# Row scales of a decoder trunk: sums over the partitions by two matmuls with a matrix of ones, and a power over 512 columns

## The chip, the cores and the metric

The kernel runs on one core of a Trainium2 chip. The metric is the device time of one execution in microseconds (us); of several executions the median is taken. Engines are named as in the profile: PE is TensorE's matmul, PEld its weight load, DVE is VectorE, ACT is ScalarE, POOL is GpSimd, SP is SyncE. L198 is line 198 of the kernel before.

## What is computed

A trunk of two decoder layers over 512 tokens with 1024 features. Each layer is a half-step SwiGLU feed-forward, a token mixer (a gated linear recurrence in the first layer, latent attention in the second), another half-step SwiGLU, and a gated embedding. An RMS norm stands ahead of every one of these, and one at the end:

```
def _rmsnorm(x, g):
    x32 = x.astype(jnp.float32)
    y = x32 * lax.rsqrt(jnp.mean(x32 * x32, axis=-1, keepdims=True) + EPS)
    return (y * g.astype(jnp.float32)).astype(x.dtype)

for li in range(DEPTH):
    g = norm_gains[li]
    x = x + 0.5 * _swiglu(_rmsnorm(x, g[0]), ffn_w_in[li, 0], ffn_w_out[li, 0])
    h = _rmsnorm(x, g[1])
    x = x + (hgrn2 mixer of h in layer 0, latent attention of h in layer 1)
    x = x + 0.5 * _swiglu(_rmsnorm(x, g[2]), ffn_w_in[li, 1], ffn_w_out[li, 1])
    gate = sigmoid(_rmsnorm(x, g[3]) @ ple_w_gate[li])
    x = x + gate * (p[li] @ ple_w_in[li])
    if li == 0:
        shared = _mla_shared_kv(x, positions, ...)   # norm, down projection, norm of 256 latents
return _rmsnorm(x, final_norm)
```

The norm's factor is one number for each token, 1/sqrt(mean of squares + EPS). Everything that follows a norm is linear until the next nonlinearity, so the kernel multiplies by the gain first, does the matmuls, and applies the factor of the token to their result.

## The kernel before, in words

**Layout.** Activations stand transposed: features on the 128 partitions, the 512 tokens along the free axis. A tensor of 1024 features is eight tiles of 128x512. A token's sum of squares is therefore a sum over the partitions and over eight tiles. The eight tiles are summed elementwise as they come (class `Stats`, L176; the squares on ACT at L183, the additions on POOL or DVE at L188). What is left is one 128x512 tile whose 128 rows must be summed.

**Matmuls.** An f32 product is made of three matmuls of halves (`mm3`, L150): each operand is split into a rounded high part `hi` (a cast on ACT, `split` L166, or L304 for weights) and the rest `lo` (a subtraction on DVE, L167, L305). Weights stream from memory in tiles of 128x1024, eight blocks of 128x128. A chain over eight blocks is 24 matmuls of 128x512 into one PSUM bank. There are eight banks: four of tag `mm` (`mm_bank`, L92) and four of tag `aux` (`aux_bank`, L95), each given out in turn, so a fifth chain on `mm` needs the first one's bank read out.

**The row factor.** `column_sums` (L211) turns the 128x512 tile by four transposes on PE (L214) into a bank, and DVE adds along the free axis (L216), which leaves 128x4: the 512 sums, one column for each 128 tokens. `Stats.columns` adds EPS on DVE (L195) and raises to the power -0.5 on POOL (L198, 128x4). `spread` (L219) broadcasts each of the four columns and transposes it back on PE (L222), and `rows` (L225) copies the bank to a tile `rb` of 128x512 on ACT (L229): each partition holds the same 512 factors. Consumers multiply a bank by `rb` on DVE, and by that free the bank.

**Where it stands.** Eight places make `rb` in this way and are touched by the change:
1. at the very start, for the first feed-forward, whose first two gate and up products are made ahead, into all four `mm` banks (`primed`, L1227);
2. to 4. at the opening of the other three feed-forwards (`plain`, L399): eight products of 24 matmuls into the `mm` banks in turn, the sums after product 0, the spread after product 1, the copy (`fresh`, L425) at the start of product 2, and then `gated` and `kept` (L387, L393), which read out two banks each time;
5. and 6. ahead of the two gated embeddings (`ple` L901 and `last` L919): eight short chains of six matmuls, then eight gate chains of 24, each read out by a multiplication with `rb` at L911;
7. the norm of the 256 shared latents (`shared`, L1036), which is worked off in steps beside the third feed-forward's first output stage;
8. ahead of the latent attention (`mla`, L1067): four chains of 24, each read out by a multiplication with `rb` at L1074 into `cq`.

A ninth place, the recurrence, uses the 128x4 form itself and stays as it was, as do the recurrence's heads, the queries' norm and the final norm.

**What sets the order.** Within a feed-forward the order on every engine is as written: `turn` (L359) takes weight tile t, does what is due at t, cuts (L299 and L304 on ACT, L300 and L305 on DVE) the tile two turns ahead, and issues the loads some turns ahead. From the fifth feature block on, pairs of blocks are multiplied with fewer products: class `Mix` (L247) prepares sums of activation halves on DVE (L262) and POOL (L264, L265), and some weight tiles are added in memory on the way in by DMAs that POOL issues (L288). Outside the feed-forwards a scheduler sets the order when the kernel is built. Each engine works through its own queue in order.

Of the kernel before, what the change touches and what calls it, by code (L numbers as in the profile page):

```python
# [28 lines left out]
EPS = 1e-6  # L29
# [28 lines left out]
def kernel(  # L58
# [12 lines left out]
    act, dve, pool, pe = nc.scalar, nc.vector, nc.gpsimd, nc.tensor  # L71
# [14 lines left out]
    def slot(s="s", dt=F32, tag="s"):  # L86
        return spool.tile([P, T], dt, tag=tag, bufs=BUFS[tag], name=name(s))
# [4 lines left out]
    def mm_bank():  # L92
        return psum.tile([P, T], F32, tag="mm", bufs=4, name=name("mm"))

    def aux_bank():  # L95
        return psum.tile([P, T], F32, tag="aux", bufs=4, name=name("aux"))
# [11 lines left out]
    ones = cpool.tile([P, 1], F32, name="ones")  # L108
    dve.memset(ones, 1.0)
    jmat = cs[:, C_J : C_J + P]  # L110


    stream = {"n": 0, "tiles": 0, "ready": [], "now": None}
# [49 lines left out]
    def split(src, scale=None, tag="s"):  # L163
        hi, lo = slot("hi", F32R, tag), slot("lo", F32R, tag)
        if scale is None:
            act.copy(hi, src)  # L166
            dve.tensor_tensor(out=lo, in0=src, in1=hi.bitcast(F32), op=ALU.subtract)  # L167
        else:
            act.activation(hi, src, AF.Copy, scale=scale)
            dve.scalar_tensor_tensor(  # L170
                out=lo, in0=src, scalar=scale, in1=hi.bitcast(F32), op0=ALU.mult, op1=ALU.subtract
            )
        return hi, lo
# [37 lines left out]
    def column_sums(src):  # L211
# [4 lines left out]
        dve.tensor_reduce(out=r, in_=pt.rearrange("p (j q) -> p j q", j=NT), axis=AX.X, op=ALU.add)  # L216
        return r

    def spread(r):  # L219
        pb = aux_bank()  # L220
        for j in range(NT):
            pe.transpose(pb[:, j * P : (j + 1) * P], r[:, j : j + 1].to_broadcast([P, P]), ident)  # L222
        return pb

    def rows(stats, sums=None):  # L225
        r = stats.columns(sums)
        pb = spread(r)
        rb = slot("rb", F32, "b")
        act.copy(rb, pb)  # L229
        return r, rb  # L230


    x = [slot("x") for _ in range(KC)]
# [86 lines left out]
    def ffn(nx, post, rb=None, primed=(), aside=None, ready=None):  # L320
# [27 lines left out]
        def at(dt, fn, late=False):  # L348
            todo.setdefault((now[0] + dt, late), []).append(fn)
# [49 lines left out]
        def plain(f0):  # L399
            xg = nx.xg[0]  # L400
            mixed = [Mix(nx, i) for i in range(KC // 2)]
            n = 2 * (PLAIN - f0)
            if f0:
                for i in range(KC // 2):
                    if i == 0:
                        mixed[0].scale()
                        mixed[0].combine()
                        mixed[0].cut(b)
                        mixed[1].scale()
                    else:  # L410
                        at(i - 1, mixed[i].combine)
                        at(i, lambda i=i: mixed[i].cut(b), True)
                        if i < KC // 2 - 1:
                            at(i - 1, mixed[i + 1].scale, True)
            else:
                for i in range(KC // 2):
                    at(max(2 * i - 1, 0), mixed[i].scale, i > 0)
                    at(2 * i, mixed[i].combine, i == 0)
                    at(2 * i + 1, lambda i=i: mixed[i].cut(b), True)
            ps = [None] * n  # L420
            r = pb = None

            def fresh():
                st["rb"] = slot("rb", F32, "b")
                act.copy(st["rb"], pb)  # L425

            for t in range(n):
                f = f0 + t // 2
                if t == 2 and not f0:
                    at(0, fresh)  # L430
                if t % 2 == 0 and t > 0:
                    at(0, lambda t=t: st.update(g=gated(ps[t - 2])))
                    at(0, lambda t=t: kept(ps[t - 1], st["g"]), True)
                if t == 2 and not f0 and ready is not None:
                    at(0, lambda: ready(st["rb"]), True)
                w = turn()
                ps[t] = aux_bank() if f0 and t < 2 else mm_bank()
                full(ps[t], w, xg, range(KC), True, True)
                if t == 0 and not f0:
                    r = nx.stats.columns(nx.stats.sums())  # L440
                if t == 1 and not f0:
                    pb = spread(r)
                now[0] += 1
            at(0, lambda: st.update(g=gated(ps[n - 2])))
            at(0, lambda: kept(ps[n - 1], st["g"]))

# [589 lines left out]
    def shared(sh, sin, cos, out):  # L1036
        tab = slot("tab", F32, "r")
        act.copy(tab[0:64, :], cos[0:64, :])
        act.activation(tab[64:128, :], sin[64:128, :], AF.Copy, scale=cs[64:128, C_SIGN : C_SIGN + 1])
        kt = slot("kt", F32, "r")  # L1040
        dve.tensor_tensor(out=kt, in0=sh.kr, in1=tab, op=ALU.mult)
        st = Stats(2)
        for c in sh.lat:
            st.add(c)
        yield
        pj = aux_bank()
        pe.matmul(pj, jmat, kt, start=True, stop=True)
        sums = st.sums()
        r = st.columns(sums)
        krope = split(pj, None, "p")  # L1050
        yield
        pb = spread(r)
        rc = slot("rb", F32, "b")
        act.copy(rc, pb)
        yield
        cn = []
        for m in range(2):
            c = slot("cn", F32, "r")
            dve.scalar_tensor_tensor(
                out=c, in0=sh.lat[m], scalar=gain(V_LAT, m), in1=rc, op0=ALU.mult, op1=ALU.mult  # L1060
            )
            cn.append(split(c, None, "p"))
            yield
        out.extend((cn, krope))


    def mla(xg, stats, cn, krope, sin, cos, post):  # L1067
        _, rb = rows(stats)
        st = Stats(4, dve)
        cq = []  # L1070
        for m in range(4):
# [156 lines left out]
    with tc.manual_schedule(engines={mybir.EngineType.SP, mybir.EngineType.PE}):  # L1228
        warm = tiny(1)
        act.activation(warm, ones, AF.Square)  # L1230
        nc.sync.dma_start(vc, vec)
        load(0)
        for i in range(4):
            stream["tiles"] += 1
            stream["n"] += WB
            raw = wpool.tile([P, WB * P], F32, tag="raw", bufs=5, name=name("raw"))
            hi = wpool.tile([P, WB * P], F32R, tag="whi", bufs=3, name=name("whi"))
            lo = wpool.tile([P, WB * P], F32R, tag="wlo", bufs=3, name=name("wlo"))
            for e in range(2):
                m = 2 * i + e  # L1240
                s = slice(e * WB * P // 2, (e + 1) * WB * P // 2)
                if i == 0:
                    nc.sync.dma_start(raw[:, s], wall[i][:, s])
                    load(m + 1)
                elif e == 0:
                    nc.sync.dma_start(raw, wall[i])
                    for k in range(m + 1, min(m + 3, KC)):
                        load(k)
                first(m)
                for n in range(2) if m == 0 else (None,):  # L1250
                    c = s if n is None else slice(s.start + n * 2 * P, s.start + (n + 1) * 2 * P)
                    act.copy(hi[:, c], raw[:, c])  # L1252
                    dve.tensor_tensor(out=lo[:, c], in0=raw[:, c], in1=hi[:, c].bitcast(F32), op=ALU.subtract)
                if m == 5:
                    nc.sync.dma_start(cs, cst)
                first.stats.add(x[m])
                if m == KC - 1:
                    sums = first.stats.sums()
                for c in range(4):
                    w = slice(s.start + c * P, s.start + (c + 1) * P)  # L1260
                    mm3(primed[c], (hi[:, w], lo[:, w]), first.xg[0][m], m == 0, m == KC - 1)
        rb = rows(first.stats, sums)[1]
    tables, held = [], []
    n1 = Next([gcol(0, 1)])

# [13 lines left out]
    n3 = Next([gcol(0, 3)])  # L1279
    ffn(n2, n3, aside=embedding(0))  # L1280
    n4 = Next([gcol(1, 0)])
    rb = rows(n3.stats)[1]
    sh = Shared()

    def both(m):
# [12 lines left out]
    mla(n5.xg[0], n5.stats, cn, krope, sin, cos, n6)  # L1298
    n7 = Next([gcol(1, 3)])
    ffn(n6, n7, aside=embedding(1))  # L1300
    last(n7.xg[0], held[1], rows(n7.stats)[1])


def _blocks(w):
# [166 lines left out]
```

## Time and profile before

| | |
|---|---|
| median of 3 runs | 2176.32 us (2176.1 to 2176.52) |
| profiled execution, own time | 2175.48 us |
| its span | 2173.7 us |
| granted TensorE clock, mean | 0.997 |
| busy: PE, DVE, ACT, POOL | 99%, 70%, 45%, 14% of the span |
| instructions on PE | 13026 |

The profile shows one execution. Its span runs from the first to the last recorded instruction; its own time is 1.8 us longer. "Busy" is the time in which an engine executes an instruction, and a duration is an instruction's own: matmuls are pipelined, so one of 128x512 shows 0.39 us while the next starts 0.23 us after it. "Idle before" is how long the engine had waited, with the instruction that ended it.

### The profile page before, as it was taken

Reading aid. Unit: us, or ns where it says so; the run is one execution under the profiler, and the core shown is the slowest. Engines: PE = TensorE matmul, PEld = TensorE weight load, DVE = VectorE, ACT = ScalarE, POOL = GpSimd, SP = SyncE. Lnnn points to the kernel's source line nnn. Section 1 sums busy time; section 2 is a strip of 40 time slices with the busy share of each in tenths; the row PEclk is TensorE's granted clock in tenths of the full one; section 3 lists DMA queues with packets and bytes.
Section 4 is the critical chain, followed back from the end, with each engine's and each line's share of the span. In section 5 each row is a group of like instructions: output and inputs, shape, how many; then the busy total and the mean of one; then the engine's idle time right before and its main releaser. Section 6 shows DMA issues by size and latency. Waiting matters only on the chain.

```text
span 2173.7 us, 32746 instructions
## 1 busy us (share of the span) xinstructions
PE 2148.8 (99%) x13026; PEld 1925.5 (89%) x13026; DVE 1522.3 (70%) x2261; ACT 968.5 (45%) x1374; POOL 313.3 (14%) x428
## 2 busy tenths in 40 slices
PE   8999999999999999999999999999999999999998
PEld 7899998898888899998888989988888888999987
DVE  6776676777786676675767757767676776775765
ACT  6354453223235343344553525446444563443543
POOL 2000001554521000001110000011110110000011
PEclk9999999999999999999999999999999999999999
DMA  5555552211123555552244655423122134654631
GB/s 192 141 157 159 144 163 96 83 69 59 68 69 105 147 159 159 141 160 101 87 119 127 172 146 157 144 91 104 59 85 91 51 105 132 151 164 126 178 104 49
DMA packets 76249, 261.46 MB, mean 120 GB/s; under 512 B 9152, under 2 KB 11328, under 8 KB 76096
## 3 DMA queue, kind: packets, MB, share of 16 engines
q1 hardware_dynamic: 64864, 220.15, 30.4%
q0 software_dynamic: 10368, 37.75, 10.1%
q8 instruction: 102, 1.67, 0.3%
q10 hardware_dynamic: 864, 1.46, 0.2%
q14 instruction: 51, 0.42, 0.1%
HBM read 253.04 MB, written 2.10 MB: 117 GB/s over the span
## 4 chain that ended last, share of the span: by engine, by line
PE 94%; DVE 3%; ACT 1%; issue 1%; DMA 0%; POOL 0%; SPq 0%; POOLq 0%; DVEq 0%; ACTq 0%
PE aux L314 19%; PE mm L151 18%; PE mm L152 18%; PE mm L153 17%; PE mm L314 14%; PE aux L152 1%; PE aux L153 1%; PE aux L723 1%; PE aux L151 1%; PE aux L1163 1%; PE aux L1138 0%; PE aux L1137 0%; ACT whi L304 0%; PE aux L214 0%; DVE wlo L305 0%
## 5 line engine op out<-in xcount | busy, mean ns | idle before, releaser
L151 PE MATMUL mm<-hi,whi 128*128 128x512 f32 x1656 | 647.1, 393 | 8.5 <-ACT whi L1252 5.6
L152 PE MATMUL mm<-lo,whi 128*128 128x512 f32 x1656 | 647.2, 391 | 1.5 <-DVE lo L380 0.9
L153 PE MATMUL mm<-hi,wlo 128*128 128x512 f32 x1656 | 646.1, 390 | 0.0
L305 DVE TENSOR_TENSOR wlo<-raw,whi 128x1024 fp32r<-128x1024 f32 x340 | 425.3, 1251 | 220.6 <-ACT whi L304 217.5
L304 ACT CAST whi<-raw 128x1024 fp32r<-128x1024 f32 x340 | 355.2, 1046 | 288.3 <-PE mm L152 163.5
L151 PEld LDWEIGHTS mm<-hi,whi 128*128 128x128 f32 x1656 | 311.3, 188 | 72.2 <-ACT whi L1252 5.6
L152 PEld LDWEIGHTS mm<-lo,whi 128*128 128x128 f32 x1656 | 311.7, 188 | 64.1 <-DVE lo L380 2.2
L153 PEld LDWEIGHTS mm<-hi,wlo 128*128 128x128 f32 x1656 | 311.5, 188 | 63.4
L314 PE MATMUL aux<-hi,whi 128*128 128x256 f32 x1152 | 328.1, 285 | 2.5 <-ACT mm L465 2.5
L314 PE MATMUL aux<-hi,wlo 128*128 128x256 f32 x1152 | 326.8, 284 | 0.2 <-DVE wlo L300 0.2
L314 PE MATMUL aux<-lo,whi 128*128 128x256 f32 x1152 | 326.5, 283 | 0.0
L314 PE MATMUL mm<-lo,whi 128*128 128x256 f32 x864 | 244.5, 283 | 0.0
L314 PE MATMUL mm<-hi,whi 128*128 128x256 f32 x864 | 244.5, 283 | 0.0
L314 PE MATMUL mm<-hi,wlo 128*128 128x256 f32 x864 | 244.4, 283 | 0.0
L314 PEld LDWEIGHTS aux<-hi,whi 128*128 128x128 f32 x1152 | 221.6, 192 | 3.3 <-ACT mm L465 2.7
L314 PEld LDWEIGHTS aux<-hi,wlo 128*128 128x128 f32 x1152 | 221.7, 192 | 0.5 <-DVE wlo L300 0.5
L314 PEld LDWEIGHTS aux<-lo,whi 128*128 128x128 f32 x1152 | 221.6, 192 | 0.5
L288 POOL DMA_DIRECT2D raw<-in_wall x72 | 62.8, 872 | 941.1 <-DMA raw<-in_wall 538.5
L129 ACT CAST whi<-raw 128x1024 fp32r<-128x1024 f32 x95 | 99.8, 1051 | 171.7 <-PE mm L152 113.1
L314 PEld LDWEIGHTS mm<-lo,whi 128*128 128x128 f32 x864 | 165.9, 192 | 0.0
L314 PEld LDWEIGHTS mm<-hi,whi 128*128 128x128 f32 x864 | 165.9, 192 | 0.0
L314 PEld LDWEIGHTS mm<-hi,wlo 128*128 128x128 f32 x864 | 165.9, 192 | 0.0
(248 smaller groups left out, 2883.6 us busy)
## 6 DMA issues: line engine op xcount, KB each, us to landing
raw<-in_wall SPq DMA_DIRECT2D x402, 512.0 KB, 3.3
raw<-in_wall POOLq DMA_DIRECT2D x72, 512.0 KB, 5.8
x<-in_xT SPq DMA_DIRECT2D x8, 256.0 KB, 6.8
qr<-hi SPq DMA_DIRECT2D x32, 64.0 KB, 2.0
qr<-lo SPq DMA_DIRECT2D x32, 64.0 KB, 2.0
out_dram<-o SPq DMA_DIRECT2D x8, 256.0 KB, 2.3
p<-in_pT ACTq DMA_DIRECT2D x4, 256.0 KB, 4.4
raw<-in_wall SPq DMA_DIRECT2D x2, 256.0 KB, 3.6
```

The source lines that it names most:

```text
L129: act.copy(hi[:, s], raw[:, s])
L151: pe.matmul(out, a[0], b[0], start=first, stop=False)
L152: pe.matmul(out, a[0], b[1], start=False, stop=False)
L153: pe.matmul(out, a[1], b[0], start=False, stop=last)
L288: nc.gpsimd.dma_start(self.raw, wall[self.plus], accum_op=ALU.add)
L304: act.copy(hi, self.raw)
L305: dve.tensor_tensor(out=lo, in0=self.raw, in1=hi.bitcast(F32), op=ALU.subtract)
L314: pe.matmul(o, w[u][:, s], b[i][v], start=first and e + i + n == 0, stop=False, skip_group_check=True)
L723: pe.matmul(sc[:, e * 192 : (e + 1) * 192].rearrange("p (i b n) -> p i b n", i=2, n=3 * m), k[:, j * P : (j + 1) * P], q4[:, :, j * nbt : ...
L1163: pe.transpose(banks[b][:, o : o + P], prob[i][:, j * P : (j + 1) * P], ident)
```

## The change

A matrix `every` of 128x128 ones is made once. At the eight places `total` splits the 128x512 tile of squares into its high and low part (ACT and DVE), and multiplies the matrix of ones with both into one bank: two matmuls of 128x512, after which every partition holds the 512 sums. `inverse` copies the bank to a tile with the scale and EPS on ACT, and POOL raises this whole tile of 128x512 to the power -0.5, which is `rb`. Gone at each place are eight transposes, the reduction to 128x4, the addition of EPS on DVE, the power over 128x4, and the copy of `rb` on ACT.

```
+    every = cpool.tile([P, P], F32R, name="every")
+    act.copy(every, ones.to_broadcast([P, P]))
...
+    def total(src=None, parts=None):
+        hi, lo = split(src, None, "r") if parts is None else parts
+        pb = aux_bank()
+        pe.matmul(pb, every, hi, start=True, stop=False)
+        pe.matmul(pb, every, lo, start=False, stop=True)
+        return pb
+
+    def inverse(pb, n, tag="b"):
+        v = slot("v", F32, "r")
+        act.activation(v, pb, AF.Copy, scale=1.0 / (n * P), bias=EPS)
+        rb = slot("rb", F32, tag)
+        pool.tensor_tensor(out=rb, in0=v, in1=mhalf[:, 0:1].to_broadcast([P, T]), op=ALU.pow)
+        return rb
...
+    def row(stats):
+        return inverse(total(stats.acc), stats.n)
...
-            def fresh():
-                st["rb"] = slot("rb", F32, "b")
-                act.copy(st["rb"], pb)
+            def fresh(pb):
+                st["rb"] = inverse(pb, KC)
...
-                if t == 2 and not f0:
-                    at(0, fresh)
...
                 w = turn()
+                if t == 0 and not f0:
+                    parts = split(nx.stats.acc, None, "r")
                 ps[t] = aux_bank() if f0 and t < 2 else mm_bank()
                 full(ps[t], w, xg, range(KC), True, True)
+                now[0] += 1
                 if t == 0 and not f0:
-                    r = nx.stats.columns(nx.stats.sums())
-                if t == 1 and not f0:
-                    pb = spread(r)
-                now[0] += 1
+                    at(0, lambda pb=total(None, parts): fresh(pb))
...
+        parts = split(st.acc, None, "r")
         yield
         pj = aux_bank()
         pe.matmul(pj, jmat, kt, start=True, stop=True)
-        sums = st.sums()
-        r = st.columns(sums)
+        rc = inverse(total(None, parts), 2)
         krope = split(pj, None, "p")
         yield
-        pb = spread(r)
-        rc = slot("rb", F32, "b")
-        act.copy(rc, pb)
         yield
...
-        _, rb = rows(stats)
+        rb = row(stats)
...
-                    sums = first.stats.sums()
+                    sums = total(first.stats.acc)
...
-        rb = rows(first.stats, sums)[1]
+        rb = inverse(sums, KC)
...
-    rb = rows(n3.stats)[1]
+    rb = row(n3.stats)
...
-    last(n7.xg[0], held[1], rows(n7.stats)[1])
+    last(n7.xg[0], held[1], row(n7.stats))
```

In the changed kernel the matmuls with ones stand at L224 and L225, the copy with EPS at L230, the power at L232; lines further down move by up to 19.

POOL's queue at the opening of the second feed-forward. Before, with the sums of activations (`tb`) for the first pairs on both sides of the power over 128x4, and a weight tile added in memory (`raw`) behind it:

```order
241 L264 TENSOR_TENSOR tb_6423<-ta_6422,be_6412 128x256
242 L265 TENSOR_TENSOR tb_6423<-tb_6423,bo_6413 128x256
243 L198 TENSOR_TENSOR t_6461<-t_6460,mhalf 128x4
244 L264 TENSOR_TENSOR tb_6513<-ta_6512,be_6478 128x256
245 L265 TENSOR_TENSOR tb_6513<-tb_6513,bo_6479 128x256
246 L288 DMA raw_6525<-in_wall 128x1024
```

The same place in the changed kernel:

```order
249 L283 TENSOR_TENSOR tb_6418<-ta_6417,be_6407 128x256
250 L284 TENSOR_TENSOR tb_6418<-tb_6418,bo_6408 128x256
251 L232 TENSOR_TENSOR rb_6457<-v_6455,mhalf 128x512
252 L283 TENSOR_TENSOR tb_6503<-ta_6502,be_6473 128x256
253 L284 TENSOR_TENSOR tb_6503<-tb_6503,bo_6474 128x256
254 L307 DMA raw_6513<-in_wall 128x1024
```

The power keeps its place among its neighbours; its output is now 128x512.

DVE's queue ahead of the first gated embedding, where the scheduler sets the order. Before, with the low parts of streamed weights (`wlo`), the reduction, and the first multiplication of a gate chain (`mm`) with `rb`:

```order
1066 L130 TENSOR_TENSOR wlo_9860<-raw_9857,whi_9859 128x1024
1067 L216 TENSOR_REDUCE t_9724<-aux_9719 128x4
1068 L195 TENSOR_SCALAR t_9717<-t_9724 128x4
1069 L130 TENSOR_TENSOR wlo_9906<-raw_9903,whi_9905 128x1024
1070 L911 TENSOR_TENSOR g_9841<-mm_9810,rb_9733 128x512
1071 L130 TENSOR_TENSOR wlo_9937<-raw_9934,whi_9936 128x1024
```

In the changed kernel, with the low part of the squares (`lo_9706`) where the reduction was:

```order
1064 L169 TENSOR_TENSOR lo_9706<-sq_9420,hi_9705 128x512
1065 L132 TENSOR_TENSOR wlo_9841<-raw_9838,whi_9840 128x1024
1066 L132 TENSOR_TENSOR wlo_9887<-raw_9884,whi_9886 128x1024
1067 L132 TENSOR_TENSOR wlo_9918<-raw_9915,whi_9917 128x1024
1068 L132 TENSOR_TENSOR wlo_9965<-raw_9962,whi_9964 128x1024
1069 L926 TENSOR_TENSOR g_9822<-mm_9791,rb_9714 128x512
```

Two more weight tiles are cut ahead of the first use of `rb`. On PE all four gate chains for which there are banks then stand ahead of the first matmul that needs a result of that use.

DVE's queue in the third feed-forward, beside which the latents are normed: `t` and `x` read out an output chain, `cn` is a latent times its factor (`rb_11014` before, `rb_10943` in the change). Before:

```order
1193 L546 SCALAR_TENSOR_TENSOR t_11045<-mm_11025,rb_10399 128x512
1194 L547 TENSOR_TENSOR x_82<-t_11045,x_82 128x512
1195 L305 TENSOR_TENSOR wlo_11052<-raw_10952,whi_11051 128x1024
1196 L1059 SCALAR_TENSOR_TENSOR cn_11055<-c_10418,vc,rb_11014 128x512
1197 L167 TENSOR_TENSOR lo_11058<-cn_11055,hi_11057 128x512
1198 L546 SCALAR_TENSOR_TENSOR t_11079<-mm_11044,rb_10399 128x512
```

In the changed kernel:

```order
1188 L561 SCALAR_TENSOR_TENSOR t_11012<-mm_10992,rb_10324 128x512
1189 L562 TENSOR_TENSOR x_84<-t_11012,x_84 128x512
1190 L324 TENSOR_TENSOR wlo_11019<-raw_10930,whi_11018 128x1024
1191 L1071 SCALAR_TENSOR_TENSOR cn_11022<-c_10392,vc,rb_10943 128x512
1192 L169 TENSOR_TENSOR lo_11025<-cn_11022,hi_11024 128x512
1193 L561 SCALAR_TENSOR_TENSOR t_11046<-mm_11011,rb_10324 128x512
```

Nothing moved here: `cn` still stands behind the fourth output chain's reading and ahead of the fifth's.

More of the change, by code (lines that the diff above doesn't have):

```diff
@@ L420, in plain @@
             ps = [None] * n
-            r = pb = None
-            def fresh():
-                st["rb"] = slot("rb", F32, "b")
-                act.copy(st["rb"], pb)
+            def fresh(pb):
+                st["rb"] = inverse(pb, KC)
             for t in range(n):
                 f = f0 + t // 2
-                if t == 2 and not f0:
-                    at(0, fresh)
                 if t % 2 == 0 and t > 0:
```

## The prediction

> **What bounds the kernel now.** I read the page first, then the waits of PE, then stretches around the eight places. From the page:
>
> ```profile
> span 2173.7 us, 32746 instructions
> ...
> PE 2148.8 (99%) x13026; PEld 1925.5 (89%) x13026; DVE 1522.3 (70%) x2261; ACT 968.5 (45%) x1374; POOL 313.3 (14%) x428
> ...
> PE 94%; DVE 3%; ACT 1%; issue 1%; DMA 0%; POOL 0%; SPq 0%; POOLq 0%; DVEq 0%; ACTq 0%
> ```
>
> PE is busy in all but 25 us of the span and is 94% of the chain that ended last. An edit gains only by taking work from PE, or out of its few gaps; it loses wherever it makes PE wait. The waits of PE for POOL are small (columns: us in total, times, longest):
>
> ```profile
> PE aux L955 <- POOL t L952: 2.1, 2, 1.1
> ...
> PE aux L222 <- POOL t L198: 0.5, 1, 0.5
> ```
>
> L955 belongs to the final norm, which stays. So at the eight places the present detour costs PE 0.5 us of waiting and its own instructions. That is also seen behind a feed-forward's opening, where PE has no gap (columns: stretch, length, then busy PE, PEld, DVE, ACT, POOL, granted clock, DMA share, GB/s):
>
> ```profile
> 680.00:700.00 20.00, 20.00 (x90) 16.57 (x89) 12.83 (x19) 10.62 (x16) 4.05 (x5) 1.00 0.42 125
> ```
>
> **What PE saves.** The timeline of PE at the first place:
>
> ```profile
> 25.33 0.39 PE L151 MATMUL mm<-hi,whi 128*128 128x512 f32 x1
> ...
> 26.46 0.39 PE L153 MATMUL mm<-hi,wlo 128*128 128x512 f32 x1
> ...
> 26.69 0.60 PE L214 MATMUL aux<-cs,sq 128*128 128x128 f32 x4
> ...
> 27.05 0.48 PE L151 MATMUL mm<-hi,whi 128*128 128x512 f32 x1
> ...
> 27.37 0.39 PE L152 MATMUL mm<-lo,whi 128*128 128x512 f32 x1
> ```
>
> Five matmuls of 128x512 take 26.46 - 25.33 = 1.13 us, 0.227 each. From 26.69 to 27.37 stand four transposes and one such matmul: the four cost 0.68 - 0.227 = 0.45 us. A place loses eight transposes (0.91) and gains two matmuls (0.45): 0.45 us saved, 3.6 us over eight places, if nothing else changes. The split of the squares (a cast and a subtraction, about 0.6 and 0.7 us) delays the sums by about 1 us where PE comes to them at once, and hides behind a product elsewhere.
>
> **What POOL gets.** This decides. The groups of POOL by shape (busy, mean ns of one, idle before):
>
> ```profile
> L188 POOL TENSOR_TENSOR sq<-sq,sq 128x512 f32<-128x512 f32 x35 | 45.4, 1296 | 316.2 <-ACT sq L183 316.2
> ...
> L683 POOL TENSOR_TENSOR T<-T 128x4 f32<-128x4 f32 x8 | 1.7, 216 | 0.6
> ```
>
> and the powers in POOL's timeline:
>
> ```profile
> 669.32 2.00 POOL L198 TENSOR_TENSOR t<-t,mhalf 128x4 f32<-128x4 f32 x1
> ...
> 1018.62 1.04 POOL L198 TENSOR_TENSOR t<-t,mhalf 128x4 f32<-128x4 f32 x1 [10.88 <-DVE t L195]
> ...
> 2162.61 0.72 POOL L952 TENSOR_TENSOR t<-t,mhalf 128x2 f32<-128x2 f32 x1 [7.40 <-ACT t L951]
> 2165.77 0.69 POOL L952 TENSOR_TENSOR t<-t,mhalf 128x2 f32<-128x2 f32 x1 [2.44 <-ACT t L951]
> ```
>
> A plain operation of two tensors takes 0.22 us for 4 columns and 1.30 for 512: 0.002 us a column. The power takes 0.71 us for 2 columns and mostly 1.02 for 4: two more columns cost 0.30 us, seventy times as much. That isn't a start-up cost, which 2 columns pay as well as 4. So each column costs about 0.152 us, with 0.40 fixed, and 512 columns D = 0.40 + 512 x 0.152 = 78 us. (1.04 against 0.69 gives 0.175 a column and D = 90.) No row shows a power on more than 4 columns. The lower bound is the plain operation, 1.3 us; the upper, 4-column price with nothing fixed, 1.02 / 4 x 512 = 130 us. I take 78: the same operation on the same engine, of which only the length changes, is nearer than another operation of the right length.
>
> [...]
>
> **What D costs at each place.** PE can go on until it needs a bank or a weight tile that waits for `rb`. "Cover" is that work, less about 1.0 us from the sums to the start of the power (a copy and the hand-overs), less what follows `rb` before PE can go on, less the loss on restart. The last is read here (columns as above):
>
> ```profile
> 50.00:60.00 10.00, 8.04 (x59) 7.45 (x57) 7.41 (x10) 4.79 (x8) 0.00 (x0) 1.00 0.17 55
> 60.00:70.00 10.00, 9.19 (x63) 8.95 (x64) 7.96 (x8) 5.03 (x7) 0.00 (x0) 0.83 0.40 126
> ```
>
> PE misses 1.96 and 0.81 us of these stretches, and in the second the granted clock averages 0.83: 1.7 us of 10 lost. I take that for each restart.
>
> *Start.* From the chain that ended last:
>
> ```profile
> 30.52 0.59 ACT rb L229
> 31.11 0.62 ACT be L257
> ```
>
> `rb` is on the chain itself, ready at 31.11. In the change the sums end at 26.69 + 7 x 0.227 = 28.3 (five other matmuls stand between the two with ones), the power starts at 29.3, `rb` comes at 29.3 + D: D - 1.8, and 1.7 for the restart: cover 0.1.
>
> *Three feed-forward openings.* Product 0 ends, the sums follow, and products 1 to 3 fill the other banks. DVE then stands at `gated`, behind it in both queues the weights of product 4. In the timeline of before:
>
> ```profile
> 674.30 0.69 DVE L389 TENSOR_TENSOR g<-mm,rb 128x512 f32<-128x512 f32 x1 [1.99 <-ACT rb L425]
> ...
> 676.12 1.04 ACT L304 CAST whi<-raw 128x1024 fp32r<-128x1024 f32 x1
> ```
>
> From `rb` to those weights' high part passes 677.16 - 674.30 = 2.9 us. Cover: 72 matmuls, 16.3, - 1.0 - 2.9 - 1.7 = 10.7 each, 32.1 for three. POOL's additions and the weight DMA queued behind the power come late too, but they are needed from product 6 on, two products (10.9 us) after PE resumes.
>
> *First embedding.* Behind the sums the change's order has six matmuls and four gate chains, 102 x 0.227 = 23.1 us; then PE needs a split x:
>
> ```profile
> 1026.40 0.69 DVE L911 TENSOR_TENSOR g<-mm,rb 128x512 f32<-128x512 f32 x1 [3.86 <-PE mm L153]
> ...
> 1032.48 0.75 DVE L170 SCALAR_TENSOR_TENSOR lo<-x,vc,hi 128x512 fp32r<-128x512 f32 x1 [0.38 <-ACT hi L169]
> ```
>
> 6.1 us after `rb`. Cover 23.1 - 1.0 - 6.1 - 1.7 = 14.3. *Last embedding:* the same 102 matmuls, then only a bank is needed, 0.7 us after `rb`: 19.7.
>
> *Latents.* DVE comes to `cn` behind the fourth output chain:
>
> ```profile
> 1153.08 0.66 PE L214 MATMUL aux<-cs,sq 128*128 128x128 f32 x4
> ...
> 1165.16 0.69 DVE L546 SCALAR_TENSOR_TENSOR t<-mm,rb 128x512 f32<-128x512 f32 x1 [2.47 <-PE mm L153]
> ...
> 1167.63 0.75 DVE L1059 SCALAR_TENSOR_TENSOR cn<-c,vc,rb 128x512 f32<-128x512 f32 x1
> ```
>
> The power would start at about 1156. Four more chains of 18 matmuls (16.3 us) fill the banks until 1181.4, and some 3 us pass from `rb` to the next reading: cover 25.4 - 3 - 1.7 = 20.7.
>
> *Attention.* Behind the sums PE has 53 matmuls (12.0 us) before the first that needs `cq`:
>
> ```profile
> 1447.60 0.69 DVE L1074 TENSOR_TENSOR cq<-mm,rb 128x512 f32<-128x512 f32 x1 [3.92 <-ACT rb L229]
> ...
> 1448.94 0.71 ACT L169 ACTIVATE hi<-cq,vc 128x512 fp32r<-128x512 f32 x1
> ...
> 1458.90 0.74 DVE L170 SCALAR_TENSOR_TENSOR lo<-cq,vc,hi 128x512 fp32r<-128x512 f32 x1
> ```
>
> The first `cq` is split 2.1 us after `rb`. The four, with no chains to wait for, are estimated at 9 us where PE has some 9 of work on them: another 1.5. Cover 12.0 - 1.0 - 2.1 - 1.5 - 1.7 = 5.7.
>
> **The sum.** Covers: 0.1 + 32.1 + 14.3 + 19.7 + 20.7 + 5.7 = 92.6. Stalls: 8 x 78.2 - 92.6 = 533 us. Less 3.6 saved: 529.4. The profiled execution's own 2175.48 (span 2173.7 and 1.8 around it) becomes 2704.9; it lies 0.8 below the median of the runs, so 2706 is forecast.
>
> **Rivals.**
>
> *The power is cheap at length.* If two and four columns are a slow remainder and a long row runs like the addition, D is 1.3 us, below every cover. `rb` at the start would come at 30.6, 0.5 earlier. The time is 2175.5 - 3.6 - 0.5 + 0.8 = 2172. For it: plain operations do cost 0.002 us a column. Against: the 0.30 us between 2 and 4. It decides below D = 5.4 us, where the start's D - 1.8 eats the 3.6 saved. This is the side that is not slower. [...] Chance 0.10; the gain of 0.19% is on the edge of what a measurement of this kernel tells from no change (about 0.2%), so half each.
>
> *The loop overlaps columns.* Two at a time in a long row, which four columns can't show: D = 39, 8 x 39 - 92.6 - 3.6 = 216, time 2392. Nothing in the rows speaks for it except that they are short. Chance 0.08. [...]
>
> *Dearer.* The power at 669.32 took 2.00 us beside busy DVE. If a long one is slowed so throughout, D is over 98 and the time over 2870: D = 110 gives 2176.3 + 880 - 96.2 = 2960. Against: DVE itself soon stands still for `rb`. Chance 0.07.
>
> **Numbers.** Forecast 0.75, for D from about 58 to 98. Its rows alone give 2706 to 2800 (D of 78 to 90), but 512 columns are far from 4, so the range takes D from 52 to 98: 8 x 52 - 96.2 above 2176.3 is 2496, 8 x 98 - 96.2 is 2864. I give 2500 to 2870, which holds the forecast and part of its neighbours, 0.8. Faster by over 0.2%: 0.05; within: 0.05; slower: 0.90.
>
> **What would show it.** Right: eight POOL rows at L232 of 128x512 near 78 us; PE idle about 76 us at the start and 55 to 72 at the others, ended by DVE or ACT work on `rb`; PE's own work 3.6 us shorter. The steps fail one by one if the power's rows are long but PE's gaps shorter by more than the covers. The whole is wrong if L232 shows a few us.

## The result, and the profile after the change

The changed kernel takes 2756.62 us (median of 4 runs, 2754.93 to 2757.99) beside 2176.37 us for the kernel before (4 runs, 2176.1 to 2176.52): the ratio is 1.2666, with a 95% interval of 1.2647 to 1.2684. That is 580 us more. The forecast was 2706, its range 2500 to 2870.

Beside the lines of the sums and of the power, which are named with the change, L153 to L155 are the product's three matmuls (L151 to L153 before), L323 and L324 the two halves of the weights' cut into a high and a low part, L333 a product's matmul of half the width (L314 before).

From the page of the profile after, the lines that were shown of before, and three strips (the span in 40 slices; busy tenths of PE and POOL, and tenths of the full clock):

```profile
span 2753.2 us, 32662 instructions
...
PE 2171.5 (79%) x12978; PEld 1933.7 (70%) x12978; DVE 1522.1 (55%) x2253; ACT 971.3 (35%) x1383; POOL 961.2 (35%) x428
...
PE   5299999999908999936365599945999936999954
...
POOL 6700003455291000193938400174111193000175
PEclk8699999999959999968677799977999967999986
...
PE 66%; POOL 24%; DVE 5%; issue 3%; ACT 2%; DMA 0%; POOLq 0%; DVEq 0%; SPq 0%; ACTq 0%
```

PE's share of the span fell from 99% to 79% with its work nearly unchanged, and POOL, which had no visible share of the chain that ended last, now has 24% of it. In the strips, PE shows a hole wherever POOL shows a 9, and the granted clock sinks there too, to 0.5 or 0.6 of the full one. DVE's and ACT's own work is as before to within 3 us. POOL's rose by 648 us. One group of the page holds that (busy, mean ns of one, idle before):

```profile
L232 POOL TENSOR_TENSOR rb<-v,mhalf 128x512 f32<-128x512 f32 x8 | 656.6, 82076 | 51.5 <-ACT v L230 51.5
```

Eight powers of 82.1 us. The waits of PE (us in total, times, longest) say who stood behind them:

```profile
PE mm L153 <- ACT whi L323: 287.2, 4, 77.0
PE mm L153 <- ACT hi L171: 73.1, 2, 72.7
PE aux L153 <- ACT hi L171: 65.2, 2, 64.4
PE mm L153 <- DVE g L926: 60.5, 1, 60.5
PE aux L333 <- ACT whi L323: 58.9, 1, 58.9
...
PE aux L225 <- DVE lo L169: 3.9, 3, 2.0
...
PE mm L153 <- ACT whi L131: 1.8, 1, 1.8
```

The name behind the arrow is the last link, not the cause: ACT cuts weights (L323) or splits `hi` (L171) only after DVE has used `rb`. The view of the line L232 itself names the first link, DVE, at four gates, two embeddings, the latents and the attention (us, times):

```profile
  DVE g L408: 318.8, 4
  DVE g L926: 125.9, 2
  DVE cn L1071: 70.3, 1
  DVE cq L1086: 68.6, 1
```

The second feed-forward opening shows the whole sequence. POOL starts the power 0.74 us after it last worked, and PE, which had filled its free banks, comes back 85.65 us later (timeline: start, duration, operation, idle before it):

```profile
747.54 81.94 POOL L232 TENSOR_TENSOR rb<-v,mhalf 128x512 f32<-128x512 f32 x1 [0.74 <-ACT v L230]
```

```profile
833.19 0.79 PE L153 MATMUL mm<-hi,whi 128*128 128x512 f32 x1 [70.08 <-ACT whi L323]
```

The windows of PE behind it (stretch, length, busy PE, granted clock, DMA share, GB/s) show the restart at half the clock:

```profile
825.00:830.00 5.00, 0.00 (x0) 0.50 0.00 0
830.00:835.00 5.00, 1.77 (x3) 0.50 0.48 77
835.00:840.00 5.00, 5.00 (x17) 0.70 0.64 179
840.00:845.00 5.00, 5.00 (x24) 1.00 0.44 97
```

The loss can be laid out by place. The delay is how much later one and the same matmul stands in the trace of after; the stall is the long wait of PE, with the short ones right behind it; the last column is how much PE's busy time rose in the same stretch.

| Stretch | delay, us | long stalls, us | PE busy, us |
|---|---|---|---|
| start | 77.1 | 77.0 | -0.3 |
| second feed-forward opening | 74.3 | 70.1 | +2.5 |
| first embedding, third opening | 148.4 | 66.2 + 70.1 | +9.7 |
| latents | 65.6 | 60.4 | +3.1 |
| attention, fourth opening | 150.9 | 72.7 + 70.1 | +6.3 |
| last embedding | 63.3 | 60.5 | +1.4 |
| sum | 579.6 | 547.1 | +22.7 |

### The profile page after: what moved, and what is told of

Read it like the earlier page. It is cut to its first block, busy times and chain, and to the rows that moved or that the text cites. A ratio compares the mean times of both kernels' runs of the same rounds, so it can differ in the third digit from the quotient of the medians.

```text
span 2753.2 us, 32662 instructions
## 1 busy us (share of the span) xinstructions
PE 2171.5 (79%) x12978; PEld 1933.7 (70%) x12978; DVE 1522.1 (55%) x2253; ACT 971.3 (35%) x1383; POOL 961.2 (35%) x428
## 3 DMA queue, kind: packets, MB, share of 16 engines
q8 instruction: 102, 1.67, 0.2%
## 4 chain that ended last, share of the span: by engine, by line
PE 66%; POOL 24%; DVE 5%; issue 3%; ACT 2%; DMA 0%; POOLq 0%; DVEq 0%; SPq 0%; ACTq 0%
POOL rb L232 24%; PE aux L333 14%; PE mm L153 12%; PE mm L154 11%; PE mm L155 11%; PE mm L333 11%; PE aux L154 1%; PE aux L155 1%; PE aux L738 1%; PE aux L153 1%; DVE wlo L324 1%; ACT whi L323 1%; DVE lo L169 1%; PE aux L1175 0%; PE aux L1149 0%
## 5 line engine op out<-in xcount | busy, mean ns | idle before, releaser
L153 PE MATMUL mm<-hi,whi 128*128 128x512 f32 x1656 | 652.3, 396 | 431.5 <-ACT whi L323 287.2
L232 POOL TENSOR_TENSOR rb<-v,mhalf 128x512 f32<-128x512 f32 x8 | 656.6, 82076 | 51.5 <-ACT v L230 51.5
L153 PEld LDWEIGHTS mm<-hi,whi 128*128 128x128 f32 x1656 | 314.4, 190 | 499.1 <-ACT whi L323 289.3
L155 PE MATMUL mm<-hi,wlo 128*128 128x512 f32 x1656 | 650.6, 393 | 1.0 <-DVE wlo L324 0.8
L324 DVE TENSOR_TENSOR wlo<-raw,whi 128x1024 fp32r<-128x1024 f32 x340 | 425.5, 1252 | 206.8 <-ACT whi L323 203.8
L323 ACT CAST whi<-raw 128x1024 fp32r<-128x1024 f32 x340 | 355.1, 1045 | 266.3 <-PE mm L154 150.6
L333 PE MATMUL aux<-hi,whi 128*128 128x256 f32 x1152 | 329.0, 286 | 61.5 <-ACT whi L323 58.9
L155 PEld LDWEIGHTS mm<-hi,wlo 128*128 128x128 f32 x1656 | 314.0, 190 | 68.8 <-DVE wlo L324 4.3
L154 PEld LDWEIGHTS mm<-lo,whi 128*128 128x128 f32 x1656 | 314.8, 190 | 66.6 <-DVE lo L399 2.4
L333 PE MATMUL aux<-hi,wlo 128*128 128x256 f32 x1152 | 327.4, 284 | 3.3 <-DVE wlo L319 1.8
L333 PE MATMUL aux<-lo,whi 128*128 128x256 f32 x1152 | 326.9, 284 | 0.0
L333 PEld LDWEIGHTS aux<-hi,whi 128*128 128x128 f32 x1152 | 222.0, 193 | 62.9 <-ACT whi L323 59.4
L333 PE MATMUL mm<-hi,whi 128*128 128x256 f32 x864 | 244.5, 283 | 0.0
L333 PE MATMUL mm<-lo,whi 128*128 128x256 f32 x864 | 244.5, 283 | 0.0
L333 PE MATMUL mm<-hi,wlo 128*128 128x256 f32 x864 | 244.4, 283 | 0.0
L333 PEld LDWEIGHTS aux<-hi,wlo 128*128 128x128 f32 x1152 | 222.0, 193 | 4.2 <-DVE wlo L319 2.4
L333 PEld LDWEIGHTS aux<-lo,whi 128*128 128x128 f32 x1152 | 222.1, 193 | 0.4
L408 DVE TENSOR_TENSOR g<-mm,rb 128x512 f32<-128x512 f32 x15 | 10.2, 686 | 318.8 <-POOL rb L232 318.8
L333 PEld LDWEIGHTS mm<-hi,whi 128*128 128x128 f32 x864 | 165.9, 192 | 0.0
```

Of the source, the lines that this page charges most:

```text
L153: pe.matmul(out, a[0], b[0], start=first, stop=False)
L154: pe.matmul(out, a[0], b[1], start=False, stop=False)
L155: pe.matmul(out, a[1], b[0], start=False, stop=last)
L232: pool.tensor_tensor(out=rb, in0=v, in1=mhalf[:, 0:1].to_broadcast([P, T]), op=ALU.pow)
L323: act.copy(hi, self.raw)
L324: dve.tensor_tensor(out=lo, in0=self.raw, in1=hi.bitcast(F32), op=ALU.subtract)
```

## The experiments

Times are medians of the executions, but widths and quarter_rows were executed once. The kernel before took 2176.22 us beside widths, start_undone, no_power and sqrt_reciprocal, 2176.57 beside quarter_rows, no_power_split_early and kept_busy, and 2176.45 beside sqrt_split_early and kept_busy_full.

The theory was the prediction's: the power costs a fixed price for each of the 512 columns, PE stands still for what the products at hand don't cover, and a restart loses a little more. The rivals to it were that something else at the same places (the ones-matmuls, the split, the copy) makes the loss, that the price lies in the number of elements, and that the loss behind a stall isn't PE's clock.

**The power's price by width (widths).** The power takes another width at each of the eight places, and the rest of the row is 1; these factors are left out of the output.

```
-        pool.tensor_tensor(out=rb, in0=v, in1=mhalf[:, 0:1].to_broadcast([P, T]), op=ALU.pow)
+        w = WIDTHS.pop(0)            # 16, 256, 64, 128, 32, 8, 384, 192
+        pool.tensor_tensor(out=rb[:, 0:w], in0=v[:, 0:w], in1=mhalf[:, 0:1].to_broadcast([P, w]), op=ALU.pow)
+        act.activation(rb[:, w:], v[:, w:], AF.Copy, scale=0.0, bias=1.0)
```

> The change, but POOL raises only the first w columns of each 128x512 tile to the power, with w = 16, 256, 64, 128, 32, 8, 384, 192 at the eight places in the program's order (start, second feed-forward, first embedding, third feed-forward, latents, attention, fourth feed-forward, last embedding); the other columns are set to 1 by ACT, so most factors are left out. Theory (a price for each column, 0.40 + 0.16 us x w): 3.0, 41.4, 10.6, 20.9, 5.5, 1.7, 61.8, 31.1 us. PE waits about 29 us at 256, 8 at 128, 49 at 384, 10 at 192 and 1 at the start, none at 64, 32 and 8: about 2280 us in all. Rival (a long row is cheaper by the column than a short one, or has a step in it): the eight powers lie on no straight line through 2, 4 and 512 columns. Rival (the waits come from the two matmuls and the split, not from the power): PE's waits don't shrink with w and the time stays near 2757.

It took 2287.44 us. POOL's groups by shape:

```profile
L236 POOL TENSOR_TENSOR rb<-v,mhalf 128x384 f32<-128x384 f32 x1 | 61.5, 61532 | 0.7 <-ACT v L232 0.7
L236 POOL TENSOR_TENSOR rb<-v,mhalf 128x256 f32<-128x256 f32 x1 | 41.1, 41137 | 0.7 <-ACT v L232 0.7
...
L236 POOL TENSOR_TENSOR rb<-v,mhalf 128x128 f32<-128x128 f32 x1 | 20.7, 20727 | 0.7 <-ACT v L232 0.7
L236 POOL TENSOR_TENSOR rb<-v,mhalf 128x64 f32<-128x64 f32 x1 | 10.6, 10552 | 12.0 <-ACT v L232 12.0
L236 POOL TENSOR_TENSOR rb<-v,mhalf 128x32 f32<-128x32 f32 x1 | 6.5, 6494 | 7.5 <-ACT v L232 7.5
L236 POOL TENSOR_TENSOR rb<-v,mhalf 128x16 f32<-128x16 f32 x1 | 2.9, 2929 | 6.2 <-ACT v L232 6.2
L236 POOL TENSOR_TENSOR rb<-v,mhalf 128x8 f32<-128x8 f32 x1 | 1.7, 1662 | 12.2 <-ACT v L232 12.2
```

From 128 to 256 columns 20.41 us are added, from 256 to 384 20.40: 0.159 a column in each, and 8 columns (0.40 + 8 x 0.159 = 1.67) lie on the same line. So the price is a straight line from 8 columns to 512. Only 32 columns lie off it, with 6.49 us where the line gives 5.5. They stood at the latents, and there the 512 columns of the changed kernel also took about 1 us more than at the other seven places (83.0 against 81.9). In the trace of after, the power began there just after DVE had begun to cut a weight tile:

```profile
1455.40 83.00 POOL L232 TENSOR_TENSOR rb<-v,mhalf 128x512 f32<-128x512 f32 x1 [7.99 <-ACT v L230]
```

```profile
1455.36 1.22 DVE L324 TENSOR_TENSOR wlo<-raw,whi 128x1024 fp32r<-128x1024 f32 x1
```

The 32 columns began in the same way, 0.04 us after a cut had begun, and the two powers over 128x4 that took 2.00 us in the kernel before began 0.66 us into one. So it is an addition of about 1 us that goes with the moment at which the power begins, and not with its width; no run changes that moment alone.

Where the power is short, PE's stall goes: PE waits 48.4 us for 384 columns, 27.9 for 256, 7.5 for 128, and none is to be seen at 64, 32 or 8. The total is 7 us over the 2280 that were expected; 5.2 us of waits for the low part of the squares (L225), which the runs without the power take up, are in it.

**A quarter of the rows (quarter_rows).** The power on 32 of the 128 partitions; the other rows' factors are 1.

```
-        pool.tensor_tensor(out=rb, in0=v, in1=mhalf[:, 0:1].to_broadcast([P, T]), op=ALU.pow)
+        act.activation(rb, v, AF.Copy, scale=0.0, bias=1.0)
+        pool.tensor_tensor(out=rb[0:32], in0=v[0:32], in1=mhalf[0:32, 0:1].to_broadcast([32, T]), op=ALU.pow)
```

> The change, but POOL raises only 32 of the 128 partitions to the power, all 512 columns of them; the other partitions get the factor 1, so most of the factors are left out. Theory (the power is paid by the column, whatever the number of partitions): POOL's rows of 32x512 take 82 us as before, and the time is that of the change, 2750 to 2762 us. Rival (paid by the element): 20 us a row, PE waits at the openings 8 us, and the time near 2270.

It took 2752.46 us, and the powers 82.0 us each:

```profile
L233 POOL TENSOR_TENSOR rb<-v,mhalf 32x512 f32<-32x512 f32 x8 | 655.9, 81990 | 57.5 <-ACT rb L232 32.1 <-PE mm L155 25.3
```

A quarter of the elements costs the same (82.0 us beside 82.1 on 128 partitions). What is paid for is the column: the 512 tokens along the row cost 82 us, on 32 partitions as on 128, and the 512 tokens laid as 128x4 mostly 1.02.

**One place undone (start_undone).** The start goes back to the old path.

```
-                    sums = total(first.stats.acc)
+                    sums = first.stats.sums()
...
-        rb = inverse(sums, KC)
+        rb = rows(first.stats, sums)[1]
```

> The change at seven places, the start as in the kernel before (transposes, power over 128x4, spread). Theory (the places add up): the start's 77.1 us by which its later landmarks moved come back: 2679 us, 2676 to 2683. Rival (the start's delay was partly hidden work that the next places pay again): less than 70 us come back, above 2686.

It took 2676.15 us (ratio to before 1.2300, interval 1.2281 to 1.2319): 80.5 us come back for one of the eight places, against the 77.1 by which its later landmarks had moved. In its trace the next place's power begins 76.2 us earlier than in the changed kernel, and 3.2 more come back at later places. So the rival falls, and this place adds to the others to within some 3 us; the other seven were not undone singly.

**No power at all (no_power).** The two matmuls, the split and the copy stay; `rb` is 1, which leaves all eight places' factors out.

```
-        pool.tensor_tensor(out=rb, in0=v, in1=mhalf[:, 0:1].to_broadcast([P, T]), op=ALU.pow)
+        act.activation(rb, v, AF.Copy, scale=0.0, bias=1.0)
```

> The change without the power: rb is set to 1 by ACT, after the copy with EPS, at all eight places, so the norms' factors are left out. Theory: everything but the power saves PE 3.6 us and no more than 4 are given back where the split delays the sums: 2170 to 2176 us, ratio to the kernel before 0.997 to 1.000. Rival (the split, the two matmuls and the moved order cost time of their own, part of the 20 us by which the forecast with the measured power still falls short): above 2180.

It took 2179.11 us, ratio 1.0012 (1.0004 to 1.0021). So the power is 577.5 of the 580 us; but what is left loses 2.7 us where the prediction had a gain of 3.6. The time lies above the theory's range and just short of the rival's. The waits of PE name the place:

```profile
PE aux L225 <- DVE lo L169: 5.6, 4, 2.0
```

and the timeline of the second opening, of PE and then of DVE, shows what stands ahead:

```profile
666.01 0.39 PE L224 MATMUL aux<-hi,every 128*128 128x512 f32 x1
668.02 0.50 PE L225 MATMUL aux<-lo,every 128*128 128x512 f32 x1 [1.62 <-DVE lo L169]
```

```profile
664.94 1.23 DVE L324 TENSOR_TENSOR wlo<-raw,whi 128x1024 fp32r<-128x1024 f32 x1 [0.95 <-ACT whi L323]
...
666.75 1.21 DVE L169 TENSOR_TENSOR lo<-sq,hi 128x512 fp32r<-128x512 f32 x1
```

The low part of the squares is made only after the cut of a weight tile, which `turn()` puts ahead of it in DVE's queue, so the second matmul with ones stops PE in the middle of a product.

**The split ahead of the weights (no_power_split_early).** As no_power, with two lines exchanged.

```
+                if t == 0 and not f0:
+                    parts = split(nx.stats.acc, None, "r")
                 w = turn()
-                if t == 0 and not f0:
-                    parts = split(nx.stats.acc, None, "r")
```

> The run without the power (all factors set to 1), with the squares' split written ahead of the weight cuts of the first turn at the three openings, where the low part came 1.6 to 2.0 us late for PE. Theory (the part without the power is a gain that these waits ate): PE's wait for the low part falls from 5.6 to under 1.5 us and the time from 2179 to 2173 to 2176. Rival (the weights, cut later by an ACT and a DVE instruction, are late in their place, or the loss was elsewhere): the time stays at 2178 or more.

It took 2171.31 us, ratio 0.9975 (0.9965 to 0.9985); the wait is gone:

```profile
PE aux L225 <- DVE lo L169: 0.5, 2, 0.3
```

7.8 us against no_power for a matter of order, more than the theory had (2173 to 2176). Of the 8.7 us between the two profiled spans, 5.1 are this wait. Another 3.4 are work that PE lost in two short stretches at half the clock, at 60.9 and 1508.2 us in the profile of no_power, which this profile doesn't have (an estimate, from two steps of 3.41 us at a clock of 0.50; PE was busy for 2146.8 us there and for 2143.9 here, at a mean clock of 0.997 and 0.998); that the order brought them isn't shown. The matmuls with ones, placed so, are worth 5.3 us (with the factors left out).

**The inverse root without POOL (sqrt_reciprocal, sqrt_split_early).** The full computation: the scaling on DVE, a square root on ACT, a reciprocal on DVE; the second kernel also has the early split.

```
-        act.activation(v, pb, AF.Copy, scale=1.0 / (n * P), bias=EPS)
+        dve.tensor_scalar(out=v, in0=pb, scalar1=1.0 / (n * P), scalar2=EPS, op0=ALU.mult, op1=ALU.add)
+        act.activation(v, v, AF.Sqrt)
...
-        pool.tensor_tensor(out=rb, in0=v, in1=mhalf[:, 0:1].to_broadcast([P, T]), op=ALU.pow)
+        dve.reciprocal(rb, v)
```

> The change with the power made by other engines: DVE scales the bank and adds EPS, ACT takes the square root, DVE the reciprocal. Theory (only the power on POOL costs): about 2 to 4 us a place including a table load on ACT, below the cover of every place but the start: 2171 to 2179 us, and faster than the kernel before if the start gains as much as it loses. Rival (any chain over 512 columns ahead of rb is late): each place still shows a wait of PE of several us and the time is above 2190.

> The full computation: sqrt_reciprocal (square root on ScalarE, reciprocal on VectorE in place of the power) with the split of the squares moved ahead of the weights' turn at the feed-forward openings, as in no_power_split_early. Theory (the two parts add: 4.0 us for the two operations of the root, from sqrt_reciprocal against no_power, and 7.8 us back from the early split, from no_power_split_early against no_power): 2183.2 - 7.8 = 2175, range 2173 to 2178, the time of the kernel before. Rival (the longer chain to rb eats what the early split gives, since both hold VectorE at the same places): 2180 to 2184.

They took 2183.2 us (ratio 1.0032, 1.0019 to 1.0045) and 2178.45 us (1.0009, 1.0000 to 1.0018). The first gives back 573 of the 580 us, but came 4 us above its range. The early split gave 4.75 us here, not 7.8, which is about the wait of L225 that it took away (5.6 with the late split, 0.5 with the early one). The second lies half a microsecond above its range. Its interval reaches 1.0000, though its median is 2 us above that of the kernel before. Of the operations the reciprocal is the long one, by the groups of sqrt_reciprocal, and each square root has a table load ahead of it:

```profile
L233 DVE RECIPROCAL rb<-v 128x512 f32<-128x512 f32 x8 | 26.8, 3353 | 11.1 <-ACT v L231 11.1
...
L231 ACT ACT_TABLE_LOAD x8 | 10.3, 1283 | 11.8 <-DVE v L230 11.7
```

With 0.69 us for the scaling and 0.63 for the root, that is 6.0 us a place (0.69 + 1.28 + 0.63 + 3.35), where 2 to 4 were expected. 3.35 of it are on DVE, which also makes the splits and cuts that PE waits for. So neither theory held in full: the parts add only in part. No kernel of these with the full computation beats the kernel before.

**PE kept busy in three stalls (kept_busy, kept_busy_full).** At the three later feed-forward openings PE runs extra matmuls into a bank that nothing reads, 296 of them in the first kernel and 310 in the second.

```
+                if t == 3 and not f0:
+                    idle = aux_bank()
+                    for _ in range(WARM):
+                        pe.matmul(idle, every, xg[0][0], start=True, stop=True)
```

> The change, with 296 extra matmuls of 128x512 (67 us, into a bank that nobody reads) behind the fourth product at the three feed-forward openings, where PE waits 70 us for the power. Theory (some 2 us are lost at each of these restarts because the granted clock falls to 0.5 while PE idles): no matmul behind the three waits takes 0.43 us instead of 0.227 and 6 to 7 us come back, 2749 to 2752 us. Rival (what is lost behind a wait is DVE's and ACT's backlog): PE waits for weights instead, and the time stays at 2755 to 2758.

> As kept_busy, with 310 instead of 296 extra matmuls at each of the three feed-forward openings, so that they end about 0.2 us after the weights of product 4 instead of 3 us before them. Theory (a restart costs more than the 1.7 us of the forecast because PE comes out of the wait at a halved clock): no gap behind the extra matmuls at the three openings, the products behind them at 0.227 us a matmul at once, and 2 to 3 us less at each: 2747 to 2752 us. Rival (the loss is the late queues of VectorE and ScalarE behind rb, not PE's clock): PE waits within the next products instead, and the time stays at 2755 to 2760.

The first took 2759.03 us, above both ranges, and decided nothing: a gap of 3 us was left, and the clock fell in it all the same. PE's timeline, and its windows:

```profile
836.24 0.80 PE L153 MATMUL mm<-hi,whi 128*128 128x512 f32 x1 [2.99 <-ACT whi L325]
```

```profile
832.00:835.00 3.00, 1.25 (x6) 1.00 0.00 0
835.00:838.00 3.00, 1.72 (x3) 0.57 0.83 116
838.00:841.00 3.00, 3.00 (x8) 0.50 0.77 236
```

The second left no gap, and the clock stayed whole:

```profile
830.00:833.00 3.00, 3.00 (x15) 1.00 0.00 0
833.00:836.00 3.00, 2.70 (x12) 1.00 0.57 79
836.00:839.00 3.00, 2.78 (x12) 1.00 0.91 247
839.00:845.00 6.00, 6.00 (x29) 1.00 0.26 100
```

Yet it took 2757.05 us, the time of the changed kernel (2756.62) within the spread of either. In its trace the way from the start of the power to the next product of half width (L333 of after) takes 108.4 us at this opening instead of 110.0, but from this power to the next one the gain is 0.6 us, at the third opening 0.0, at the fourth 0.2. Over the whole profile PE's busy time, less the extra 930 x 0.227 = 211, is 2166.9, so 4.6 us less than the 2171.5 of after; the rest of its span, 2754.3 - 2166.9 = 587.4, is 5.7 more than the 581.7 of after. At these three places the rival held: PE waits more for late work instead, over the whole profile 2.4 us instead of 0.8 for the low parts of weights from DVE (L155) and 4.5 instead of 2.5 for a bank from ACT (L333 of after). So behind `rb` PE's slow matmuls and the late queues of DVE and ACT cover one another. The halved clock is real, but its removal is worth at most 0.6 us at each of them. At the other five places it was not tried.

## Why the prediction was right, and where its terms were off

**What decides.** The prediction named POOL's power of 512 columns as the step on which all hangs, and priced it from the two rows with 2 and 4 columns. That held: without the power (no_power) 577.5 of 580 us are gone. The rival of a cheap power falls (82.1 us, not 1.3), and so does that of a loop that overlaps columns, as the widths lie on one line down to 8. The dearer one (over 98) doesn't come either: all eight powers took 81.9 to 83.0 us, with DVE at work for at most 8.2 us of each. What it was read from, 2.00 us beside a busy DVE where the others over 128x4 took 1.01 to 1.04, was 1 us added once and not a slower column: over 512 columns the addition was no larger (83.0 beside 81.9).

**The power's price, mis-sized by 4 us.** The step "each column costs about 0.152 us, with 0.40 fixed" had the fixed part right and the column 5% low, since it rested on 0.30 us between two rows of about 1 us: 0.1595 measured, D = 82.07 instead of 78.2. That it came so near has some luck in it: the prediction's other reading of the same rows, 0.175 a column and D = 90, would have been 8 us too dear. Eight times 3.87 is 31.0 of the 50.6 us by which the forecast was low.

**The covers.** With D = 82.07 they foretell idle times of 80.3 at the start, 69.7 at each opening, 66.1, 59.7, 74.7 and 60.7 at the others. Measured are 77.0, 70.1, 66.2, 60.4, 72.7 and 60.5. Seven of the eight are within 2 us, the start within 3.3. So the method (what PE can do until it needs a bank or a tile that waits, less what follows `rb`) carries the result, and its errors partly cancel: the foretold ones add up to 550.6 us, the measured ones to 547.1.

**What stands ahead of the sums.** The step that failed is that the split of the squares "hides behind a product elsewhere". It doesn't at the openings: L225 waits for `lo` behind the weight cut on DVE. no_power gives 2179.1 where the sum without stalls was 2172.8: 6.3 us, in runs that spread over 5.5, and 5.6 of them are these waits. no_power_split_early shows that the order makes them: they fall to 0.5, and 7.8 us come back. In the changed kernel itself they are 3.9 us. The saving of 3.6 itself was therefore right in kind (5.3 with the early split).

**The restart.** The rest of the 50.6 can be read from the table. PE's busy time rose by 22.7 us where the prediction has 10.0 (eight restarts of 1.7 less the 3.6 saved): 12.7 more. Delays less stalls less busy time leave 579.6 - 547.1 - 22.7 = 9.8 us of short waits, for which the prediction has no term; the 3.9 at L225 are among them. The stalls are 3.5 shorter. So 31.0 + 12.7 + 9.8 - 3.5 = 50.0, and 0.6 is the difference between profiled executions and medians.

The restart's 1.7 us was too small. In the trace of after PE is busy for 48.0 us at half the clock, in that of before for 5.8; half of the difference, 21.1 us or 2.6 a place, is work that PE didn't do. The first embedding and the third opening have the largest share (PE busy 9.7 us longer). There PE stops twice, as its timeline shows:

```profile
1257.80 1.65 PE L153 MATMUL aux<-hi,whi 128*128 128x512 f32 x3 [64.36 <-ACT hi L171]
...
1260.53 0.63 PE L155 MATMUL aux<-hi,wlo 128*128 128x512 f32 x1
...
1263.52 0.50 PE L153 MATMUL mm<-hi,whi 128*128 128x512 f32 x1 [1.79 <-ACT whi L131]
...
1266.08 0.63 PE L154 MATMUL mm<-lo,whi 128*128 128x512 f32 x1
1266.51 0.63 PE L155 MATMUL mm<-hi,wlo 128*128 128x512 f32 x1
...
1268.38 0.39 PE L154 MATMUL mm<-lo,whi 128*128 128x512 f32 x1
1268.61 0.40 PE L155 MATMUL mm<-hi,wlo 128*128 128x512 f32 x1
```

After the long stall and after the short one, the matmuls stand 0.43 us apart (1266.08, 1266.51) and only then 0.23. How much of the 21.1 us a full clock would bring back stays open for the five places that kept_busy_full leaves alone; at the three openings the clock alone is worth less than 1 us each.

**Beside the forecast's list of signs.** Eight rows at L232 near 78 us: 82.1. Idle about 76 at the start: 77.0. 55 to 72 elsewhere: 58.9 to 72.7. PE's own work 3.6 us shorter: wrong, 22.7 longer, which is for the most part the half clock hiding the saving, and not the matmuls with ones, as PE's busy time in no_power (2146.8 against 2148.8 before) shows.

## What to carry to other kernels

Before an operation is widened to save a layout step, price it by the column from rows of the same operation at two lengths: a power on POOL that mostly took 1.02 us on 128x4, and held PE up for 0.5 us in all, took 82.1 on 128x512 and stopped PE for 58.9 to 77.0 us at each place, though a plain addition of that size took 1.30 there. Then go to each place where it stands and count the work that the bound engine still has until it needs the result; the wait is the price less this cover, and here it was foretold to within 3.3 us at each place. An edit that saves matmuls can lose more by the place of its helper operations in another engine's queue than it gains (2.7 us lost in no_power), and two exchanged lines can turn that round (5.3 gained in no_power_split_early).

## What the runs showed of the hardware that was not expected

- POOL's power costs 0.40 us and 0.159 for each column, in a straight line from 8 to 512 columns, and the same on 32 partitions as on 128 (81.99 and 82.08 us). The powers that began while DVE was in the middle of a weight cut took 1.0 us more: 83.0 instead of 81.9 in the trace of after, 2.00 instead of 1.02 twice in that of before, 6.49 instead of 5.5 in that of widths. One over 128x4 that began in a multiplication of DVE over 128x512 took 1.43 (1903.38 in after), one that began in a subtraction of that size 1.04 (1156.38 in before).
- The granted clock changes on a grid of 3.41 us: in the traces of before and after, 12 of the 14 stretches at half the clock are a whole number of such steps long, 1 to 23 of them; the other two are the last of each trace, which run past the end. Pauses of PE that were shorter than a step came with half the clock too: one of 3.0 us (kept_busy, the windows above) and one of 1.8 us not long after a restart. These are two steps of the grid in the trace of after, with PE busy for 1.62 us of the first and at half the clock in the second:

```profile
1261.26:1264.67 3.41, 1.62 (x6) 1.00 0.00 0
1264.67:1268.08 3.41, 3.41 (x9) 0.50 0.52 154
```

Behind the pause of 3.0 us nine matmuls of 512 columns in a row start 0.43 us after the one before instead of 0.227 (from 838.52 in kept_busy), behind that of 1.8 us five (from 1266.08 in after). A pause of 1.53 us in the latent attention was followed by such a step in after (0.50 from 1947.34 to 1950.75) and not in before (from 1504.09, clock 1.00), so the length of a pause alone does not decide.
- A reciprocal of 128x512 took DVE 3.35 us, nearly five times the scaling of the same tile (0.69, by its group in sqrt_reciprocal).
